# FFN up-projection in seven products of halves and four token blocks, in place of eight products and three blocks

## The chip, the cores and the metric

The kernel runs on one core of a Trainium2 chip. The metric is the device time of one execution in microseconds. Three runs of the kernel before took 3087.99, 3089.96 and 3090.21 us; the median, 3089.96 us, is the time before. The rows shown below come from one further execution under the profiler.

The engines by their names in the profile: PE is the matrix engine (PEld its weight loads), DVE the vector engine, ACT the scalar engine, POOL the GpSimd engine, SP the queue that issues most DMAs. Each engine works through its own instructions strictly in the order in which the kernel wrote them.

## The reference, cut to what matters

One decoder layer over 2048 prompt tokens and 8 sample tokens. The head part (a gated MLP over chunks, and an attention over a compressed cache) adds to `x`; then comes the part that is changed, a feed-forward net with a causal convolution of width 3:

```
def conv_ffn(x, conv_prev, g_ffn, w_up, w_conv, b_conv, w_down):
    h = rmsnorm(x, g_ffn)
    up = h @ w_up                                  # 1024 -> 2 x 2816 (gate and value)
    xp = jnp.concatenate([conv_prev, up], axis=1)
    c = b_conv
    for k in range(CONV_W):
        c = c + xp[:, k:k + T] * w_conv[k]
    gate, val = c[..., :D_FF], c[..., D_FF:]
    y = (jax.nn.silu(gate) * val) @ w_down         # 2816 -> 1024
    return y, xp[:, -(CONV_W - 1):]
```

The final result is `rmsnorm(x + y)`. All is float32.

## The kernel before, in words

Each float32 operand of a large product is split into a high and a low part in a shorter format, and a product is made of three matmuls: high by high, high by low, low by high (`mm3`, line 78). `split_to` (line 124) makes the two parts: ACT copies the high part out (line 86), and DVE or POOL subtracts it from the source (line 126).

The stages follow one another: latent projections (0 to 300 us), the gated MLP (300 to 560), the attention of the prompt (576 to 1106), the output projection (1106 to 1343), the feed-forward part (1343 to the end). In the gated MLP, `finish` writes its output to memory already split, a high and a low copy (`a_sp`, line 1021 on); the output projection reads both (`load_a`, line 1106).

The feed-forward part takes the tokens in three blocks (`BL`: 344 + 344, 344 + 344 and 424 + 256 tokens). For a block, `load_h2` brings the 1024 input rows in and splits them; each of 22 steps `fi` (in `up`, line 1769) then makes 128 gate and 128 value columns for both halves of the block. One half of one of these is 24 matmuls, 8 slices of the input by three, into one PSUM bank. `conv` (line 1567) takes the bank: DVE multiplies by the tokens' norm factor (line 1572), ACT writes two columns of the tokens before (line 1573), starts the convolution (line 1574) and saves the last two columns (line 1575), and DVE adds the other two taps (line 1577). `glu` applies the gate: silu on ACT, a product on DVE (line 1586), the high part on ACT, the low part on DVE. Three banks (`pu`) go round among the up-projections, three (`pd`) among the down-projections.

After two steps the down-projection of this pair is done, in eight pieces `m` for each half; a piece is six matmuls and a DVE addition to `y` (line 1597). `PIECES` says where among the next pair's up-projections a piece stands. The weights come in through POOL's DMA queue; ACT and POOL split them (1024 columns at a time, `split_w`, line 1366). At a block's end `ending` makes the last pair's down-projection, and the next block's input is prepared meanwhile.

Beside this runs the attention of the eight sample tokens over 16,384 cached positions: `fill` (line 869) counts the columns that were fed to PE and, when enough have passed, writes one more step of it between two matmuls. A step reads 4 pages for each of four samples; in the feed-forward part one stands after each 10.25 us of counted columns (at one column per 1/2.4 ns). It ends with the second block. In the third, `late` normalises the finished blocks' output. Nothing reorders what is written: the order in the code is the order on each engine.

## Time and profile before

| what | value |
| --- | --- |
| time, median of three runs | 3089.96 us |
| the profiled execution, its own time | 3097.86 us |
| its span, first to last instruction | 3096.1 us |
| PE busy, share of the span | 97% |
| DVE, ACT, POOL busy | 55%, 42%, 35% |
| feed-forward part | 1343 to 3096 us |
| PE's granted clock, mean | 0.987 |

"Busy" is the share of the span in which at least one instruction of the engine ran. PE's matmuls overlap one another, so what one matmul costs is read from the distance of starts in a row of them, not from the duration of one. In the groups of instructions a row gives busy time, mean duration of one, and the engine's idle time just ahead of them with the engine that ended it.

### The profile page before, as it was taken

Reading aid. Unit: us, or ns where it says so; the run is one execution under the profiler, and the core shown is the slowest. Engines: PE = TensorE matmul, PEld = TensorE weight load, DVE = VectorE, ACT = ScalarE, POOL = GpSimd, SP = SyncE. Lnnn points to the kernel's source line nnn. Section 1 sums busy time; section 2 is a strip of 40 time slices with the busy share of each in tenths; the row PEclk is TensorE's granted clock in tenths of the full one; section 3 lists DMA queues with packets and bytes.
Section 4 is the critical chain, followed back from the end, with each engine's and each line's share of the span. In section 5 each row is a group of like instructions: output and inputs, shape, how many; then the busy total and the mean of one; then the engine's idle time right before and its main releaser. Section 6 shows DMA issues by size and latency. Waiting matters only on the chain.

```text
span 3096.1 us, 66568 instructions
## 1 busy us (share of the span) xinstructions
PE 2992.7 (97%) x23814; PEld 2697.3 (87%) x23814; DVE 1716.6 (55%) x3595; ACT 1293.6 (42%) x2986; POOL 1088.1 (35%) x1097
## 2 busy tenths in 40 slices
PE   8999999999999989999999999999999999999997
PEld 7898788688887779879999999899898989999997
DVE  6466333577787754444444444554444456666666
ACT  5333333577778742233332322343332334444443
POOL 4342122422233234343333323333232334444442
PEclk9999999999999999999999999999999999999999
DMA  5446766788865789989777777949898845333333
GB/s 165 138 160 211 217 186 194 210 222 225 222 172 136 193 238 256 241 242 226 203 211 231 239 231 240 277 113 222 209 218 217 213 140 173 109 95 112 112 93 81
DMA packets 354070, 587.76 MB, mean 190 GB/s; under 512 B 60879, under 2 KB 261230, under 8 KB 353742
## 3 DMA queue, kind: packets, MB, share of 16 engines
q1 hardware_dynamic: 277520, 375.31, 43.6%
q0 software_dynamic: 56416, 197.65, 22.7%
q10 hardware_dynamic: 19806, 10.55, 1.1%
q8 instruction: 191, 3.13, 0.4%
q14 instruction: 137, 1.12, 0.1%
HBM read 515.50 MB, written 67.82 MB: 188 GB/s over the span
## 4 chain that ended last, share of the span: by engine, by line
PE 74%; DMA 8%; DVE 6%; issue 5%; ACT 4%; POOL 2%; SPq 1%; ACTq 0%; DVEq 0%; POOLq 0%
PE up L76 27%; PE dp L76 13%; PE s L76 5%; PE op L76 5%; PE sc L76 4%; PE po L76 4%; PE o L76 3%; PE t L1224 3%; PE pu L76 2%; PE pv L76 2%; DMA cn<-in_cN 2%; DMA ct<-in_cT 1%; SPq L66 1%; DVE c L1577 1%; PE pj L76 1%
## 5 line engine op out<-in xcount | busy, mean ns | idle before, releaser
L76 PE MATMUL up<-h,wu 128*128 128x344 f32 (+2 forms) x6336 | 1070.0, 321 | 6.1 <-DVE h L1550 2.1
L76 PEld LDWEIGHTS up<-h,wu 128*128 128x128 f32 x6336 | 1002.4, 189 | 22.0 <-issue 6.4
L126 POOL TENSOR_TENSOR wu<-wraw,wu 128x1024 fp32r<-128x1024 f32 x132 | 315.3, 2389 | 694.2 <-ACT wu L86 668.0
L1577 DVE SCALAR_TENSOR_TENSOR c<-up,gn,c 128x344 f32<-128x344 f32 (+2 forms) x528 | 302.6, 573 | 293.5 <-ACT halo L1575 284.2
L1573 ACT ACTIVATE up<-halo 128x2 f32<-128x2 f32 x264 | 46.1, 175 | 709.5 <-DVE up L1572 705.6
L76 PE MATMUL dp<-gh,wdh 128*128 128x344 f32 (+1 forms) x960 | 311.1, 324 | 12.3 <-ACT gh L86 6.4
L76 PE MATMUL dp<-gl,wdh 128*128 128x344 f32 (+1 forms) x960 | 306.9, 320 | 0.3
L76 PE MATMUL dp<-gh,wdl 128*128 128x344 f32 (+1 forms) x960 | 306.9, 320 | 0.0
L1597 DVE TENSOR_TENSOR y<-y,dp 128x344 f32<-128x344 f32 (+1 forms) x480 | 227.5, 505 | 118.5 <-PE dp L76 116.4
L1572 DVE TENSOR_TENSOR up<-up,R 128x344 f32<-128x344 f32 (+2 forms) x264 | 137.3, 520 | 232.6 <-PE up L76 232.4
L76 PE MATMUL s<-k,q 96*128 96x512 f32 (+2 forms) x960 | 254.0, 375 | 6.3 <-DMA k<-kr_sp 2.5
L126 POOL TENSOR_TENSOR wdl<-wraw,wdh 128x1024 fp32r<-128x1024 f32 x66 | 159.7, 2420 | 243.9 <-ACT wdh L86 237.7
L126 DVE TENSOR_TENSOR pl<-t,ph 128x512 fp32r<-128x512 f32 (+1 forms) x320 | 194.0, 606 | 50.7 <-ACT ph L86 47.1
L86 ACT ACTIVATE ph<-t 128x512 fp32r<-128x512 f32 (+1 forms) x320 | 170.2, 532 | 108.7 <-PE t L1224 104.2
L1212 ACT ACTIVATE S<-S,nm 128x512 f32<-128x512 f32 (+2 forms) x320 | 208.0, 650 | 7.1 <-POOL nm L1204 7.1
L76 PEld LDWEIGHTS s<-k,q 96*128 96x128 f32 x960 | 169.0, 191 | 45.4 <-DVE S L1200 6.6
L76 PEld LDWEIGHTS dp<-gh,wdh 128*128 128x128 f32 x960 | 181.3, 189 | 19.6 <-DVE y L1597 9.7
L76 PEld LDWEIGHTS dp<-gl,wdh 128*128 128x128 f32 x960 | 180.8, 188 | 2.3 <-DVE gl L126 1.4
L76 PEld LDWEIGHTS dp<-gh,wdl 128*128 128x128 f32 x960 | 180.9, 188 | 0.7
L1224 PE MATMUL t<-cst,S 128*128 128x128 f32 x1088 | 173.7, 274 | 2.3 <-DVE pl L126 2.2
L1574 ACT ACTIVATE c<-up,gn 128x344 f32<-128x344 f32 (+2 forms) x264 | 168.4, 638 | 8.9
L1224 PEld LDWEIGHTS t<-cst,S 128*128 128x128 f32 x1088 | 133.2, 140 | 35.0 <-DVE pl L126 7.1
(388 smaller groups left out, 5121.4 us busy)
## 6 DMA issues: line engine op xcount, KB each, us to landing
ct<-in_cT SPq DMA_DIRECT2D x1024, 144.0 KB
cn<-in_cN SPq DMA_DIRECT2D x1024, 128.0 KB
wraw<-in_w_up POOLq DMA_DIRECT2D x132, 512.0 KB, 4.8
wraw<-in_w_down POOLq DMA_DIRECT2D x66, 512.0 KB, 5.0
q_sp<-qs SPq DMA_DIRECT2D x48, 256.0 KB
ft<-x_sp SPq DMA_DIRECT2D x64, 172.0 KB
xt<-in_xT SPq DMA_DIRECT2D x16, 512.0 KB
kn_sp<-qs SPq DMA_DIRECT2D x32, 256.0 KB
```

What stands on the lines that cost most here:

```text
L66: return self.eng.dma_start(out=o, in_=i)
L76: pe.matmul(out, lhsT=w, rhs=x, start=start, stop=stop)
L86: act.activation(out, in_, AF.Copy)
L126: (lo_eng or dve).tensor_sub(lo, src, f(hi))
L1212: act.activation(s, s, AF.Exp, scale=SCALE, bias=d["nm"][:, qb:qb + 1], accum_out=d["ls"][:, qb, r:r + 1])
L1224: pe.transpose(p[:, (qb - q0) * 128:(qb - q0) * 128 + 128], d["S"][qb, kb // 4][:, ks], ident)
L1572: dve.tensor_mul(p[:, 2:2 + m], p[:, 2:2 + m], RT[b][:, o:o + m])
L1573: act.activation(p[:, 0:2], halo[:, ix, :], AF.Copy)
L1574: act.activation(c[:, 0:m], p[:, 2:2 + m], AF.Identity, scale=w[2], bias=g(B_CONV, ix))
L1577: dve.scalar_tensor_tensor(out=c[:, 0:npr], in0=p[:, j:j + npr], scalar=w[j], in1=c[:, 0:npr], op0=ALU.mult, op1=ALU.add)
L1597: dve.tensor_add(y, y, p[:, 0:nn])
```

## The change

The up-projection of a step `fi` is written as a product of two-by-two blocks: the weights' rows of blocks are gate and value, their columns the two halves of the input rows; the input's columns of blocks are the two token halves. Such a product of blocks needs eight products of halves; by Strassen's scheme (in Winograd's form) it is done with seven, of sums and differences of blocks. `split_w` makes the seven weight forms, of which four sums or differences are new work (two on DVE, two on POOL), and each form is split by ACT and POOL. `load_h2` makes the seven input forms once for a block, and multiplies the norm factor in there, so that `conv` no longer does. `up` adds the seven results together on DVE: `s1` (an ACT copy of the first result), `u2` and `u3` are kept in SBUF, the other sums are made in the PSUM banks.

A block has 512 tokens in halves of 256 (the last 520, halves of 260), and there are four blocks. A product of halves is 12 matmuls. The PSUM banks have fixed roles now: a, b, c and e for the seven products in the order a, b, a, b, c, b, e, one buffer each, and two for the down-projection, whose pieces are 512 tokens wide (in the last block two of 260). Weights come through SP's DMA queue, not POOL's. The gated MLP's output is stored once and split when it is read. The new query of the samples' second half is placed later in the sample stream, and `cnew` shares a buffer with the query.

```
-                split_to(a[:, 0], a[:, 1], p)
+                a = sb.tile([128, 4, 128], F32, tag="as" if c < 7 else ("hh", "hl")[tt], bufs=2, name="as")
+                copy(a, p)
...
                 if c < 7 or tt:
                     for a, t0 in todo:
-                        for i in range(2):
-                            aq.dma_start(out=a_sp[i, :, t0:t0 + 128].rearrange("(k p) t -> p k t", p=128), in_=a[:, i])
+                        aq.dma_start(out=a_sp[:, t0:t0 + 128].rearrange("(k p) t -> p k t", p=128), in_=a)
...
     def load_a(ci, tiles):
         MA[ci] = tiles
-        for i in range(2):
-            gq.dma_start(out=tiles[i], in_=a_sp[i, :, ci * CP:ci * CP + CP].rearrange("(k p) t -> p k t", p=128))
+        gq.dma_start(out=tiles[1], in_=a_sp[:, ci * CP:ci * CP + CP].rearrange("(k p) t -> p k t", p=128))
+
+    def split_a(ci, eng):
+        hi, lo = MA[ci]
+        copy(hi, f(lo))
+        eng.tensor_sub(lo, f(lo), f(hi))
 
...
+    FORMS = ("B11", "T2", "B21", "T3", "T1", "T4", "B22")
+    PIECES = ((0, 0, 1, 1, 1, 0, 0), (1, 1, 1, 1, 1, 0, 0))
+    BL = [(0, 256), (512, 256), (1024, 256), (1536, 260)]
+    NB, AHEAD = len(BL), 5
...
+    def form(src):
+        w = kslot([128, 2, 4, 128], "wu", F32R)
+        split_to(w[:, 0], w[:, 1], src, pool)
+        return w
...
+        A21, A22 = VAL[2 * q], VAL[2 * q + 1]
+        if j == 0:
+            src = A11
+        elif j == 1:
+            TMP[1] = sb.tile([128, 4, 128], F32, tag="t1", bufs=1, name="t1")
+            TMP[2] = sb.tile([128, 4, 128], F32, tag="t2", bufs=1, name="t2")
+            dve.tensor_add(TMP[1], A21, A22)
+            dve.tensor_sub(TMP[2], TMP[1], A11)
+            src = TMP[2]
+        elif j == 2:
+            src = A12
+        elif j == 3:
+            pool.tensor_sub(A21, A11, A21)
+            pool.tensor_sub(TMP[2], A12, TMP[2])
+            src = A21
         else:
-            gq.dma_start(out=t.rearrange("p j m n -> p j (m n)"),
-                         in_=A["w_down"][w[2] * 128:(w[2] + 2) * 128, w[3] * 512:w[3] * 512 + 512].rearrange("(j p) n -> p j n", p=128))
-        raw[w] = t
-
-    def split_w():
-        if at["split"] == len(order):
-            return
-        w = order[at["split"]]
-        at["split"] += 1
-        if w is None:
-            return
-        src = raw.pop(w)
-        if w[0] == "u":
-            hi, lo = (kslot([128, 8, 128], "wu", F32R) for _ in range(2))
...
+        wts[i] = form(src)
+        if j == 4:
+            later.append(load_g)
...
+            if i % (2 * NF) == 2 * NF - 2 or i == 4 * NU // 2 - 1:
+                w = kslot([128, 2, 2, 2, 128], "wd", F32R)
+                hi, lo = w[:, 0], w[:, 1]
+            else:
+                hi, lo = (sb.tile([128, 2, 2, 128], F32R, tag=t, name=t) for t in ("wdh", "wdl"))
+            split_to(hi, lo, DR.pop(i), pool)
+            wts["d", i] = hi, lo
+            dlater.append(load_d)
+
...
-        pd = mkpool(Fx, "f_pd", 3, PSUM)
+        pu = mkpool(Fx, "f_pu", 1, PSUM)
+        pd = mkpool(Fx, "f_pd", 2, PSUM)
         halo = one.tile([128, 2 * NF, 2], F32, name="halo")
...
+            hi("B21")
+            yield
+            lo("T2", dve)
+            hi("T3")
...
+            lo("T3", dve)
+            hi("T4")
+            yield
+            lo("T1", dve)
+            lo("T4", dve)
+            hi("B22")
+            yield
+            lo("B22", pool)
+            yield
 
         def load_y(b):
-            c0, n0, n1 = BL[b]
+            c0, hm = BL[b]
             for m in range(8):
...
-            c = sb.tile([128, 424], F32, tag=f"c{gv}", bufs=3 - gv, name=f"c{gv}")
-            dve.tensor_mul(p[:, 2:2 + m], p[:, 2:2 + m], RT[b][:, o:o + m])
+            c = sb.tile([128, 260], F32, tag=f"c{gv}", bufs=2, name=f"c{gv}")
             act.activation(p[:, 0:2], halo[:, ix, :], AF.Copy)
             act.activation(c[:, 0:m], p[:, 2:2 + m], AF.Identity, scale=w[2], bias=g(B_CONV, ix))
             act.activation(halo[:, ix, :], p[:, npr:npr + 2], AF.Copy)
...
                     dve.tensor_add(y, y, p[:, 0:nn])
                     fill(6 * nn / 2.4)
-                    yield
+                if m % 2:
+                    dlater.append(split_d)
+                yield
 
         def wide(name):
...
         def up(b, fi, it, side, slow, hs):
-            halves = ends(b)
-            cg = []
-            for gv in range(2):
-                wh, wl = wts.pop(("u", b, fi, gv))
-                both = fi == gv == 0
-                for h, (o, m) in enumerate(halves):
-                    at_k, at_end = (ENDING if fi == NF - 1 and b == 2 else PIECES)[4 * (fi % 2) + 2 * gv + h]
-                    if not (both and o):
-                        ps = [pu.tile([128, 512], F32, tag="u", name="up") for _ in range(1 + both)]
-                        for k in range(8):
-                            for p, (o_, m_) in zip(ps, halves if both else ((o, m),)):
-                                mm3(p[:, 2:2 + m_], [(wh[:, k, :], wl[:, k, :], h2[b][0][k][:, o_:o_ + m_], h2[b][1][k][:, o_:o_ + m_])], k == 0, k == 7)
...
-                                take(side, 1 + both)
-                            if k == 3 and not both:
...
+
+            def prod(j, name):
+                w, (xh, xl) = wts.pop(7 * q + j), H[FORMS[j]]
+                ps[name] = p = pu.tile([128, 512], F32, tag="u" + name, name="up")
+                for k in range(4):
+                    mm3(p[:, 2:2 + hm], [(w[:, 0, k, :], w[:, 1, k, :], xh[:, k, 0:hm], xl[:, k, 0:hm])], k == 0, k == 3)
+                    fill(3 * hm / 2.4)
+                return p[:, 2:2 + hm]
+
+            def rest(j):
+                todo, later[:] = later[:], []
+                dtodo, dlater[:] = dlater[:], []
+                for fn in todo + dtodo:
+                    fn()
+                while at["w"] <= 7 * q + j + AHEAD and at["w"] < 7 * NU:
+                    split_w()
+                take(it, PIECES[odd][j])
+                take(side, 1)
+                take(slow, 1)
+                take(hs, 1)
+
+            s1, u2, u3 = (sb.tile([128, 260], F32, tag=t, bufs=1, name=t)[:, 0:hm] for t in ("s1", "u2", "u3"))
+            copy(s1, prod(0, "a"))
+            rest(0)
+            dve.tensor_add(u2, s1, prod(1, "b"))
+            rest(1)
+            p = prod(2, "a")
+            dve.tensor_add(p, s1, p)
+            cg = conv(b, fi, 0, ps["a"], 0, hm)
+            rest(2)
+            dve.tensor_add(u3, u2, prod(3, "b"))
+            rest(3)
+            p = prod(4, "c")
+            dve.tensor_add(u2, u2, p)
+            dve.tensor_add(p, u3, p)
+            rest(4)
+            p = prod(5, "b")
+            dve.tensor_add(p, u3, p)
+            cv = conv(b, fi, 1, ps["b"], 0, hm)
+            if odd:
+                take(it, 99)
+            gt = [sb.tile([128, 520], F32R, tag=t, bufs=3, name=t) for t in ("gh", "gl")]
+            run(glu(cg, cv, gt, 0, hm))
+            cv = conv(b, fi, 1, ps["c"], hm, hm)
+            rest(5)
+            p = prod(6, "e")
+            dve.tensor_add(p, u2, p)
+            cg = conv(b, fi, 0, ps["e"], hm, hm)
+            last = glu(cg, cv, gt, hm, hm)
+            next(last)
+            if not (b == NB - 1 and fi == NF - 1):
+                run(last)
+            rest(6)
             return gt, last
 
...
+        for b in range(NB):
...
+                if fi == NF - 1 and b < NB - 1:
+                    if b == NB - 2:
+                        drain()
+                    hs = load_h2(b + 1)
+                gt, last = up(b, fi, it, side, slow if fi else none, hs)
...
-                act.activation(sb.tile([128, 1], F32, tag="t1", bufs=1, name="t1"), epst, AF.Sqrt)
+            split_d()
+            if b < NB - 1:
+                it = ending(b, (before, gt))
+                for _ in range(8):
+                    take(it, 1)
+                    take(hs, 1)
```

ACT's order, at the end of a step and the start of the next. In the kernel before, a stretch of a step's two value halves (`wu` is a weight's high part, `up<-halo` starts a conv, `c` its first tap or, `c<-c`, the silu, `gh` the gated result's high part):

```order
L86 ACTIVATE wu<-wraw 128x1024
L1573 ACTIVATE up<-halo 128x2
L1574 ACTIVATE c_26294<-up,gn 128x344
L1575 ACTIVATE halo<-up 128x2
L1585 ACTIVATE c_26098<-c_26098 128x344
L86 ACTIVATE gh<-c_26294 128x344
L1573 ACTIVATE up<-halo 128x2
L1574 ACTIVATE c_26450<-up,gn 128x344
L1575 ACTIVATE halo<-up 128x2
L1585 ACTIVATE c_26138<-c_26138 128x344
L86 ACTIVATE gh<-c_26450 128x344
L86 ACTIVATE wu<-wraw 128x1024
```

And in the changed kernel, the end of a step with odd `fi` (the convolutions of banks c and e, `wdh` a down weight's high part, `s` the next step's `s1`):

```order
L1741 ACTIVATE up<-halo 128x2
L1742 ACTIVATE c_24734<-up,gn 128x256
L1743 ACTIVATE halo<-up 128x2
L86 ACTIVATE wdh<-draw 128x512
L86 ACTIVATE wu<-vraw 128x512
L1741 ACTIVATE up<-halo 128x2
L1742 ACTIVATE c_24763<-up,gn 128x256
L1743 ACTIVATE halo<-up 128x2
L1753 ACTIVATE c_24763<-c_24763 128x256
L86 ACTIVATE gh<-c_24734 128x256
L86 ACTIVATE wu<-t_24665 128x512
L86 ACTIVATE s_24778<-up 128x256
```

Two weight copies stand between the two convolutions now, and the copy of the next step's first product, which gives bank a free for its third, stands behind the whole of the gate.

POOL's order. In the kernel before, among the up-projections (`wu` and `wdl` are low parts):

```order
L126 TENSOR_TENSOR wu<-wraw,wu 128x1024
L66 DMA wraw<-in_w_up 128x1024
L126 TENSOR_TENSOR wu<-wraw,wu 128x1024
L66 DMA wraw<-in_w_down 128x2x512
L126 TENSOR_TENSOR wu<-wraw,wu 128x1024
```

In the changed kernel, at the end of a step with odd `fi` (lines 1397 and 1398 are the two differences of the next weight forms):

```order
L126 TENSOR_TENSOR wu<-graw,wu 128x512
L126 TENSOR_TENSOR wdl<-draw,wdh 128x512
L1397 TENSOR_TENSOR vraw<-graw,vraw 128x512
L1398 TENSOR_TENSOR t_26786<-graw,t_26786 128x512
L126 TENSOR_TENSOR wu<-vraw,wu 128x512
L126 TENSOR_TENSOR wu<-t_26785,wu 128x512
```

The DMA issues are gone from POOL, its subtractions are half as wide and more than twice as many, and the difference `vraw`, which ACT's copy `wu<-vraw` reads, stands behind the low part of a down weight.

## Rows read from the trace of the kernel before

**Rows 1.** The page, its first two lines (span; busy us, share, instructions).

```profile
span 3096.1 us, 66568 instructions
...
PE 2992.7 (97%) x23814; PEld 2697.3 (87%) x23814; DVE 1716.6 (55%) x3595; ACT 1293.6 (42%) x2986; POOL 1088.1 (35%) x1097
```

**Rows 2.** Busy by stage: length; PE, PEld, DVE, ACT, POOL; PE clock, DMA share, GB/s.

```profile
300.00:560.00 260.00, 251.01 (x1918) 202.79 (x1917) 90.95 (x207) 90.36 (x162) 62.53 (x85) 0.97 0.71 206
1140.00:1342.00 202.00, 195.68 (x1698) 179.36 (x1691) 79.44 (x117) 43.96 (x92) 83.05 (x106) 0.97 0.92 245
1400.00:1900.00 500.00, 500.00 (x4857) 477.63 (x4856) 237.24 (x498) 150.91 (x359) 169.58 (x113) 1.00 0.78 224
2690.00:3050.00 360.00, 354.09 (x2251) 344.92 (x2250) 227.69 (x471) 149.38 (x359) 157.95 (x112) 1.00 0.35 103
```

**Rows 3.** The chain of waits, whole run; columns: start, us, what.

```profile
363.44 5.58 PE pv L76 x24
...
1328.35 14.40 PE op L76 x120
...
1440.67 11.33 PE up L76 x72
...
2684.32 11.22 PE up L76 x72
```

**Rows 4.** Timeline of PE around 1702 us; columns: start, us, engine, what.

```profile
1702.19 1.95 PE L76 MATMUL sc<-ct,qz 128*32 128x128 f32 x64
...
1704.30 2.15 PE L76 MATMUL up<-h,wu 128*128 128x344 f32 x12
```

**Rows 5.** Timeline of DVE and ACT, one half of 256, third block.

```profile
2923.46 0.43 DVE L1572 TENSOR_TENSOR up<-up,R 128x256 f32<-128x256 f32 x1
...
2923.98 0.17 ACT L1573 ACTIVATE up<-halo 128x2 f32<-128x2 f32 x1
2924.19 0.56 ACT L1574 ACTIVATE c<-up,gn 128x256 f32<-128x256 f32 x1
2924.65 0.16 ACT L1575 ACTIVATE halo<-up 128x2 f32<-128x2 f32 x1
2924.85 0.99 DVE L1577 SCALAR_TENSOR_TENSOR c<-up,gn,c 128x248 f32<-128x248 f32 x2 [0.96 <-ACT halo L1575]
...
2925.94 0.41 ACT L1585 ACTIVATE c<-c 128x256 f32<-128x256 f32 x1
...
2927.06 0.42 DVE L1586 TENSOR_TENSOR c<-c,c 128x256 f32<-128x256 f32 x1
...
2927.51 0.42 ACT L86 ACTIVATE gh<-c 128x256 fp32r<-128x256 f32 x1 [1.16 <-DVE c L1586]
...
2927.96 0.42 DVE L126 TENSOR_TENSOR gl<-c,gh 128x256 fp32r<-128x256 f32 x1 [0.48 <-ACT gh L86]
```

**Rows 6.** Groups by form, 0 to 1345 us, POOL, ACT and DVE.

```profile
L126 POOL TENSOR_TENSOR vl<-gv,vh 128x512 fp32r<-128x512 f32 x16 | 20.7, 1291 | 24.5 <-ACT vh L86 24.5
...
L86 ACT ACTIVATE ph<-t 128x256 fp32r<-128x256 f32 x32 | 12.3, 384 | 10.9 <-PE t L1224 10.4
...
L86 ACT ACTIVATE vh<-gv 128x512 fp32r<-128x512 f32 x16 | 10.1, 631 | 27.6 <-DVE gv L1058 27.6
...
L1115 DVE TENSOR_TENSOR rd<-rd 128x512 f32<-128x512 f32 x7 | 4.9, 700 | 10.4 <-ACT rd L1114 10.4
```

**Rows 7.** Timeline of POOL and DVE around 1370 us.

```profile
1369.58 2.38 POOL L126 TENSOR_TENSOR wu<-wraw,wu 128x1024 fp32r<-128x1024 f32 x1
1369.84 2.50 DVE L1586 TENSOR_TENSOR c<-c,c 128x344 f32<-128x344 f32 x1 [0.61 <-ACT c L1585]
```

**Rows 8.** Timeline of PE around a gap at 1107 us.

```profile
1106.23 0.92 PE L76 MATMUL op<-ma,wo 128*128 128x256 f32 x6
1111.24 6.79 PE L76 MATMUL op<-ma,wo 128*128 128x256 f32 x42 [4.09 <-DVE rdT L1256]
```

**Rows 9.** Busy time and clock behind this gap; columns as in rows 2.

```profile
1110.00:1114.00 4.00, 2.76 (x13) 2.76 (x14) 3.76 (x6) 0.00 (x0) 1.97 (x4) 0.67 0.19 41
```

More of the change, by code (lines that the diff above doesn't have):

```diff
@@ L765, in sample_stream @@
             yield 1500
+            if s == 0:
+                qz = yield from place_q(1)
             def turned(p0):
@@ new lines, in build, with load_g, load_v @@
+    PIECES = ((0, 0, 1, 1, 1, 0, 0), (1, 1, 1, 1, 1, 0, 0))
+    BL = [(0, 256), (512, 256), (1024, 256), (1536, 260)]
+    NB, AHEAD = len(BL), 5
+    NU = NB * NF
+    GATE, VAL, TMP, wts, later, dlater = {}, {}, {}, {}, [], []
+    at = {"g": 0, "v": 0, "w": 0, "dl": 0, "ds": 0}
+    def load_g():
+        q = at["g"]
+        at["g"] += 1
+        if q < NU:
+            GATE[q] = qslot([128, 8, 128], "graw")
+            (sp if q else gq).dma_start(out=GATE[q], in_=A["w_up"][q % NF, 0])
+    def load_v():
+        if not at["v"]:
+            at["v"] = 2
+            t = qslot([128, 8, 128], "vraw")
+            gq.dma_start(out=t, in_=A["w_up"][0, 1])
+            VAL[0], VAL[1] = t[:, 0:4], t[:, 4:8]
+            return
+        q, a = divmod(at["v"], 2)
+        at["v"] += 1
+        if q < NU:
+            VAL[2 * q + a] = t = sb.tile([128, 4, 128], F32, tag="vr", bufs=3, name="vraw")
+            sp.dma_start(out=t, in_=A["w_up"][q % NF, 1, :, 4 * a:4 * a + 4, :])
@@ new lines, in load_h2 @@
+                lo("T2", dve)
+                for n, eng in (("B21", dve), ("T3", pool), ("T1", dve), ("T4", pool), ("B22", dve)):
+                    hi(n)
+                    lo(n, eng)
+                return
+            free("B11")
+            sp.dma_start(out=raw("B11"), in_=src(0, 4, 0))
+            R = load_r()
+            yield
+            free("T2")
+            yield
+            free("B21")
+            sp.dma_start(out=raw("B21"), in_=src(4, 4, 0))
+            yield
+            free("T3")
@@ new lines, in load_h2 @@
+            sp.dma_start(out=raw("T3"), in_=src(0, 4, 1))
+            yield
+            free("T1")
+            for k in range(4):
+                scale(raw("B11", k), raw("B11", k), k, 0)
+            yield
+            free("T4")
+            xs = temps()
+            for i in range(2):
+                sp.dma_start(out=xs[i], in_=src(4 + 2 * i, 2, 1))
+            for k in range(4):
+                scale(raw("B21", k), raw("B21", k), 4 + k, 0)
+            yield
+            free("B22")
@@ new lines, in load_h2 @@
+            for k in range(4):
+                scale(raw("T3", k), raw("T3", k), k, 1)
+            hi("B11")
+            yield
+            sub("T1", "T3", "B11", dve)
+            yield
+            for k in range(4):
+                scale(b22(k), b22(k), 4 + k, 1)
+            lo("B11", pool)
+            yield
+            sub("T2", "B22", "T1", dve)
+            hi("T2")
+            yield
+            sub("T4", "B21", "T2", pool)
+            sub("T3", "B22", "T3", dve)
+            hi("B21")
@@ new lines, in ending @@
+            for i in (0, 1, 2, 3, 4, 8, 9, 5, 10, 11, 12, 13, 6, 14, 7, 15):
+                m = i % 8
+                if i < 8:
+                    ps[m] = bank(m)
+                    part(m, 0)
+                    continue
+                part(m, 1)
+                y = Y[b][m][:, 0:512]
+                dve.tensor_add(y, y, ps.pop(m))
+                sp.dma_start(out=x3_sp[m * 128:(m + 1) * 128, BL[b][0]:BL[b][0] + 512], in_=y)
+                if m % 2 and m != 5:
+                    split_d()
+                    while dlater:
+                        dlater.pop(0)()
@@ L1637, in late @@
+            for o in range(0, 1536, 512):
+                cols = slice(o, o + 512)
                 t = load(0)
@@ L1894, in build @@
-            assert next(slow, 0) == 0
-            it, slow = none, late() if b == 1 else none
+            take(it, int(TA))
+            r0 = root(0)
+            for _ in range(4):
+                take(r0, 1)
+                take(it, 1)
+            take(r0, 9)
+            take(it, 99)
+            for m in DA0:
+                scale(0, m, dve, sp)
+            half = [scale_pool(0, m, sp) for m in range(8) if m not in DA0 + DA1]
+            for t in half:
+                next(t)
+            r1 = root(1)
@@ L1896, in build @@
+            take(r1, 1)
+            for t in half:
+                next(t, 0)
+            take(r1, 99)
+            for m in DA1:
+                scale(0, m, dve, sp)
+            for m in range(8):
+                scale(1, m, pool if m in DA2 else dve, aq if m % 2 else sp)
     smp.close()
```

413 lines of the change are left out of this document (204 added, 209 removed).

## Prediction

> **What bounds the kernel now.** I read the page's busy shares first: PE works for 97% of the span [rows 1], so PE's stream is the time. The table by stage says where that holds: in the first block of the feed-forward part PE is busy for all 500 of 500 us, in the third for 354 of 360, with DVE at 47% and 63%, POOL at 34% and 44% [rows 2]. The other engines are servants with slack: what they do ends in time, and only columns fed to PE count. The change takes PE work away and gives DVE, ACT and POOL more, so the question is whether they still end in time. For that I read the chain of waits for the price of a matmul [rows 3] and the timeline of one convolution for the delay from a full bank to the finished gate [rows 5].
>
> **PE work removed.** Cost of a matmul by its width, from runs in the chain of waits [rows 3]: 256 columns 14.40/120 = 0.120 us; 344 columns 11.33/72 = 0.157; 424 and 256 in equal number 11.22/72 = 0.156 on average; 512 columns 5.58/24 = 0.2325. Before, up: 4224 x 0.157 + 2112 x 0.156 = 994 us. Now each of 88 steps has 7 products of 12 matmuls: 7392 x 0.120 = 887 (a quarter of them have 260 columns: +3). Down: 3168 matmuls at 0.157 and 0.156 = 497 before; now 1584 of 512 columns and 1056 of 260: 368 + 128 = 496. The sum is -105 us; of the nominal 1/8 of the columns a part goes into 1056 more matmuls. Were this all, the time would be 3098 - 105 = 2993. The sample stream's steps, 2.11 us each on PE [rows 4], stay as many; in a pair of steps 28.16 us of columns are counted now, so 28.16/10.25 = 2.75 sample steps stand in a pair, 5.8 us.
>
> **The new wait.** Call the end of a step's sixth product (bank b) zero. Bank a takes the step's first and third product, so the next step's third waits for the ACT copy `s1`. PE has only the seventh product and the next step's first and second before it: 3 x 12 x 0.120 = 4.3 us; after an even step two down pieces of 6 x 0.2325 = 1.4 us more, 7.1 us. But ACT and DVE have three convolutions and two gates to do first, in a fixed order, each waiting for the other. From one half of 256 tokens [rows 5]: a DVE operation on a bank 0.42; ACT's three operations until DVE starts 0.87; the two taps 0.99; silu 0.41, product 0.42, high part 0.42. Walk: sum for bank b done at 0.5; its taps from 1.5 to 2.5; product 2.9; high part 3.35; ACT then takes bank c, its taps run from 4.1 to 5.1, and only behind them comes DVE's sum for bank e, 5.5; taps from 6.45 to 7.45; silu 7.9; product 8.3; high part 8.75; a weight copy, 0.63 [rows 6]; `s1`, 0.38 [rows 6]: 9.6 us. PE has 4.3 or 7.1 us of work for it, and on average one sample step per pair.
>
> After an odd step POOL enters the chain. Between c and e ACT copies a down weight (to 4.6); POOL's low part of it and then the difference `vraw` are 1.29 us each [rows 6], to 7.2; ACT's copy `wu<-vraw` waits for that and ends at 7.85, and e's convolution, due at 5.6, starts there: `s1` at 11.9. After an even step the first gate's product meets POOL at the same two differences. Rows show what that costs: a product of 344 that started 0.26 us behind a POOL subtraction took 2.50 us, and ended 0.38 us after it [rows 7], against 0.42 for 256 alone [rows 5]. For a POOL operation of 1.29 I take half of it: 10.2.
>
> From `s1` on, the third to sixth product and three pieces take 4 x 1.44 + 3 x 1.4 = 10 us on PE, so that a step is about 20 to 22 us and sample steps, where PE alone would need 16.
>
> Per pair in blocks one to three PE stands still for (11.9 - 4.3) + (10.2 - 7.1) - 2.1 = 8.6 us.
>
> The clock adds to this. Behind a gap of 4.09 us at 1107 us [rows 8] the granted clock of the next stretch is 0.67 [rows 9], and 42 matmuls took 6.79 us, where 42 x 0.120 = 5.04: 1.75 us lost, 1.2 in place of 2.4 GHz for a part of them. The gap after an odd step (7.6) is longer than that one, the other (3.1) shorter; I take 1.75 once and half of it once, 2.6 per pair.
>
> 33 pairs x 11.2 = 370; the first pair of each of these blocks has no pieces and costs 3.3 more: 380. Block four has no sample steps, pieces of 12 x 0.120 = 1.45 us, and two short DVE operations for the sample columns in banks c and e (1 us a step; unmeasured at this place, 0.5 to 1.5): per pair 7.5 + 2.9 + 2 + 3.5 (both gaps are long there) = 15.9, times 11 = 175. Sum 555.
>
> **The rest.** At a block's end the last gate of the odd step is late by some 10 us and DVE has seven subtractions of 1024 columns for the next block's input, while PE has only the down-projection of the last pair. I put 10 us for each of three block ends and 10 for the start, where the norm factor is now on the way to the first matmul: 40, within 0 (all of it in PE's shadow) and 80. Weights by SP's queue, which has pages to issue: the weights are asked for about a step ahead, and PE needs 512 tokens' worth of them more slowly than before; nothing, 0 to 20. The gMLP output stored once: PE idles for 9.0 us in that stage and 6.3 in the output projection [rows 2], so nothing above 15 can come back; split when read, it puts an ACT copy and a POOL subtraction of 1024 columns before each chunk's norm, beside eight pieces of 2.9 us of PE work; between -15 and +10, I take 0. The sample's query and `cnew` moved: nothing.
>
> **Sum.** 3098 - 105 + 555 + 40 = 3588 for a profiled execution; the profiled one before was 8 us above the median of the runs, so 3580.
>
> **Rivals.**
>
> A lighter chain: the same wait, but POOL does not come into it and the gaps leave the clock alone. Then both tails are 9.6: (19.2 - 11.4 - 2.1) x 33 + 10 + 7.5 x 11 = 281, no cost at block ends, 3098 - 105 + 281 - 8 = 3266. For it: POOL is busy for only 22 x 1.29 = 28.4 us of a pair of 40 or more. Against it: the order puts POOL's two operations into the odd tail whatever its share, and the clock did fall behind a gap. This floor needs no unmeasured number.
>
> A heavier one: DVE falls behind too. In the middle of a step it has two sums of weights, 0.70 each alone [rows 6]; if each meets a POOL operation by half, 1.3 us a step reaches the sixth sum, 114 in all; the other half of the clock's price (30) and the normalisation of finished blocks in block four (33) come on top: 3757. Against it: that stretch is PE's, and after a gap PE is slower itself, so much of the 1.3 is covered.
>
> Not slower: PE never waits, since the tails are covered; 2985. The place is bank a, and it decides at a tail of 4.3 to 7.1 us plus a sample step; the walk would have to be too long by half. For it: before, the same convolutions are wholly hidden, with PE at 500 of 500 us [rows 2]. Against: there the four halves of a step come 3.8 us or more apart, as PE makes them (24 x 0.157), now three come within 1.44 us and ACT may not pass one by. In this case block four has a bound of its own, DVE and POOL together: if their operations on two SBUF tensors can't overlap [rows 7], a pair has 28.4 of POOL and 8 x 0.42 + 4 x 0.70 = 6.2 of such DVE work, 34.6 us, against 264 x 0.1217 = 32.1 on PE; 11 x 2.5 = 28 us, and the time is 3013. The Trainium skill, "SBUF — State Buffer", section "SBUF: two separate sides", states it as a rule: a VectorE operation with two SBUF inputs and a GpSimd operation that reads SBUF share one pair of ports, and the later one is blocked for the whole of the earlier. The 2.50 us row agrees with it.
>
> That the change does not do what it says is no case: the order shows 12 matmuls a product, seven products a step.
>
> **Chances.** The forecast's chain (3400 to 3700) 0.6; the lighter 0.18; the heavier 0.13; not slower 0.09. The range from 3290 to 3750 leaves out the last, the lowest part of the lighter and the top of the heavier. This kernel's runs agree within 0.1%, so 0.2% or 6 us can be told from no change: faster 0.08, the same 0.01, slower 0.91.
>
> **What would show it.** Right: PE's share falls to about 80%, its idle time stands ahead of the third product of each step (waiting for ACT's `s1`), longer after odd steps; ACT waits for POOL at `wu<-vraw` in odd steps for some 2.5 us, for DVE at `gh` and `up`; the clock's mean falls to about 0.93; steps in the middle of blocks one to three last about 24 us on average, up matmuls start 0.120 us apart within a product. Wrong: PE stays above 95%, or its idle time stands elsewhere (behind DMA, at block ends, at pieces). Were ACT's copy `s1` to end less than 7 us after the sixth product, the whole sum falls.

## The result and the profile after

The changed kernel takes 3665.23 us (median of 4 runs, 3660.63 to 3672.88), the kernel before 3090.09 (4 runs, 3087.99 to 3092.2): 1.186 times as long, 95% interval 1.184 to 1.189. Forecast were 3580 us, range 3290 to 3750. Each time of an experiment below is that of one run where no number of runs stands with it.

The head of the page after (span, then busy us, share and instructions), to be read against [rows 1]:

```profile
span 3662.3 us, 71440 instructions
...
PE 3040.3 (83%) x24340; PEld 2651.6 (72%) x24340; DVE 2120.6 (58%) x4367; ACT 1627.3 (44%) x4025; POOL 1770.5 (48%) x1665
```

PE now stands still for 3662.3 - 3040.3 = 622 us; before it was 103 [rows 1]. It is also busy for 48 us more, although the counted work fell by 105: some 153 us went into slower matmuls, most of it to the lower clock, as shown further down. These two, 518 and 48, are the whole change of the span.

The table by stage (length; PE, PEld, DVE, ACT, POOL; PE clock, DMA share, GB/s) says where. The first window is the gated MLP, where only the store of its output is changed, and has its like in the first line of [rows 2]; the others lie in the first block and in block four:

```profile
300.00:560.00 260.00, 252.66 (x1938) 203.30 (x1937) 83.69 (x198) 92.81 (x166) 65.30 (x87) 0.97 0.67 196
1400.00:1900.00 500.00, 406.78 (x3624) 355.52 (x3624) 266.30 (x541) 196.23 (x530) 280.10 (x222) 0.89 0.63 187
3100.00:3550.00 450.00, 311.69 (x2224) 303.90 (x2225) 277.85 (x603) 191.77 (x502) 254.12 (x195) 0.83 0.30 99
```

PE was busy for 500 of 500 us in the first block [rows 2], now for 407, and DVE, ACT and POOL are at 62% or less in each of the windows: no engine is busy all the time. The view of waits names who waits for whom (engine, its instruction's line, releaser: us in total, times, longest):

```profile
PE up L76 <- ACT s L86: 366.5, 73, 11.7
...
ACT wu L86 <- POOL vraw L1397: 106.3, 40, 4.2
...
PE dp L76 <- DVE y L1769: 69.9, 20, 7.6
...
DVE t L1391 <- DMA vraw<-in_w_up: 32.5, 11, 5.6
```

The first line is the forecast's wait: 366.5 us ahead of `up` for ACT's copy `s1`. All of it stands ahead of a step's third product (input form `B21h`), as the group of these matmuls shows (busy us, mean ns, idle time ahead and its releaser):

```profile
L76 PE MATMUL up<-B21h,wu 128*128 128x256 f32 (+1 forms) x704 | 211.0, 376 | 366.5 <-ACT s L86 366.5
```

The second line is ACT's wait for POOL's difference, 2.66 us each; all 40 stand between the sixth product of an odd step and the next `s1`. The third, down pieces that wait for DVE, was not in the forecast; all but 0.3 us of it is in block four.

Here is one odd tail of the third block, from the timeline (start us, us, engine, what), first PE, then ACT, POOL and DVE:

```profile
2716.00 0.28 PE L76 MATMUL up<-T4h,wu 128*128 128x256 f32 x1
2716.12 0.29 PE L76 MATMUL up<-B22h,wu 128*128 128x256 f32 x1
...
2728.14 0.58 PE L76 MATMUL up<-B21h,wu 128*128 128x256 f32 x1 [5.52 <-ACT s L86]
2728.52 0.42 PE L76 MATMUL up<-B21l,wu 128*128 128x256 f32 x1
2728.74 0.63 PE L76 MATMUL up<-B21h,wu 128*128 128x256 f32 x2
```

```profile
2719.28 0.42 ACT L86 ACTIVATE gh<-c 128x256 fp32r<-128x256 f32 x1 [1.36 <-DVE c L1754]
...
2720.31 0.63 ACT L86 ACTIVATE wdh<-draw 128x512 fp32r<-128x512 f32 x1
2723.55 0.63 ACT L86 ACTIVATE wu<-vraw 128x512 fp32r<-128x512 f32 x1 [2.61 <-POOL vraw L1397]
2724.09 0.16 ACT L1741 ACTIVATE up<-halo 128x2 f32<-128x2 f32 x1
...
2726.88 0.42 ACT L86 ACTIVATE gh<-c 128x256 fp32r<-128x256 f32 x1 [0.49 <-DVE c L1754]
...
2727.72 0.36 ACT L86 ACTIVATE s<-up 128x256 f32<-128x256 f32 x1
```

```profile
2721.02 1.28 POOL L126 TENSOR_TENSOR wdl<-draw,wdh 128x512 fp32r<-128x512 f32 x1 [4.93 <-ACT wdh L86]
2722.25 1.27 POOL L1397 TENSOR_TENSOR vraw<-graw,vraw 128x512 f32<-128x512 f32 x1
...
2724.70 1.26 POOL L126 TENSOR_TENSOR wu<-vraw,wu 128x512 fp32r<-128x512 f32 x1
```

```profile
2716.32 0.43 DVE L1987 TENSOR_TENSOR up<-u,up 128x256 f32<-128x256 f32 x1 [0.73 <-PE up L76]
...
2724.93 1.00 DVE L1745 SCALAR_TENSOR_TENSOR c<-up,gn,c 128x256 f32<-128x256 f32 x2 [3.14 <-ACT halo L1743]
```

The sixth product's last matmul (form `T4h`) starts at 2716.00 and ends at 2716.28. Counted from there, the first high part is done at 3.4 us, ACT's copy of the down weight at 4.7, POOL's difference at 7.2, ACT's copy that waited for it at 7.9, the second high part at 11.0, `s1` at 11.8. The prediction's walk had 3.35, 4.6, 7.2 and 7.85 for the first four and 11.9 for the last. PE had a sample step beside its 4.3 us of work here and still stood still for 5.52 us.

Behind that gap the granted clock is at its lower level: 0.50, 1.2 GHz in place of 2.4, in the 4 us after it (the column ahead of the last two). The price: matmuls of 256 columns start 0.22 us apart there (2728.52 to 2728.74) in place of 0.12. It is the case of [rows 8, 9] again.

```profile
2728.00:2732.00 4.00, 3.86 (x15) 3.67 (x16) 0.85 (x2) 1.63 (x6) 3.66 (x3) 0.50 1.01 224
```

### The profile page after: what moved, and what is told of

It reads as the page before. It is cut to its first block, busy times and chain, and to the rows that moved or that the text cites. A ratio compares the mean times of both kernels' runs of the same rounds, so it can differ in the third digit from the quotient of the medians.

```text
span 3662.3 us, 71440 instructions
## 1 busy us (share of the span) xinstructions
PE 3040.3 (83%) x24340; PEld 2651.6 (72%) x24340; DVE 2120.6 (58%) x4367; ACT 1627.3 (44%) x4025; POOL 1770.5 (48%) x1665
## 5 line engine op out<-in xcount | busy, mean ns | idle before, releaser
L126 POOL TENSOR_TENSOR wu<-t,wu 128x512 fp32r<-128x512 f32 x264 | 345.4, 1308 | 510.5 <-ACT wu L86 486.2
L1745 DVE SCALAR_TENSOR_TENSOR c<-up,gn,c 128x256 f32<-128x256 f32 (+2 forms) x704 | 340.7, 484 | 372.5 <-ACT halo L1743 359.9
L76 PE MATMUL up<-B21h,wu 128*128 128x256 f32 (+1 forms) x704 | 211.0, 376 | 366.5 <-ACT s L86 366.5
L76 PE MATMUL dp<-gh,wdh 128*128 128x512 f32 (+1 forms) x800 | 305.4, 382 | 70.4 <-DVE y L1769 69.9
L126 POOL TENSOR_TENSOR wdl<-draw,wdh 128x512 fp32r<-128x512 f32 x171 | 228.6, 1337 | 254.9 <-ACT wdh L86 249.3
L76 PE MATMUL dp<-gl,wdh 128*128 128x512 f32 (+1 forms) x800 | 299.4, 374 | 0.0
L76 PE MATMUL dp<-gh,wdl 128*128 128x512 f32 (+1 forms) x800 | 297.2, 371 | 0.0
L126 POOL TENSOR_TENSOR wu<-vraw,wu 128x512 fp32r<-128x512 f32 x176 | 229.8, 1306 | 116.5 <-ACT wu L86 116.5
L126 POOL TENSOR_TENSOR wu<-graw,wu 128x512 fp32r<-128x512 f32 x176 | 228.2, 1297 | 103.6 <-ACT wu L86 103.6
L1741 ACT ACTIVATE up<-halo 128x2 f32<-128x2 f32 x352 | 59.3, 169 | 477.2 <-DVE up L1987 217.1
L1769 DVE TENSOR_TENSOR y<-y,dp 128x512 f32<-128x512 f32 (+1 forms) x400 | 226.6, 577 | 59.4 <-PE dp L76 58.5
```

What stands on the lines that cost most here:

```text
L76: pe.matmul(out, lhsT=w, rhs=x, start=start, stop=stop)
L126: (lo_eng or dve).tensor_sub(lo, src, f(hi))
L1741: act.activation(p[:, 0:2], halo[:, ix, :], AF.Copy)
L1745: dve.scalar_tensor_tensor(out=c[:, 0:npr], in0=p[:, j:j + npr], scalar=w[j], in1=c[:, 0:npr], op0=ALU.mult, op1=ALU.add)
L1769: dve.tensor_add(y, y, p[:, 0:nn])
```

## The experiments

The theory is the prediction's: bank a waits for `s1`, and `s1` stands behind a serial chain of ACT and DVE into which POOL comes in odd steps; the clock falls behind the gaps. Its rivals: the mere amount of ACT's and DVE's work, or a clock that falls for another reason. "Tail" is the time from the end of the sixth product to the end of the next `s1`, a mean over the fifth to twentieth step of a block; in the changed kernel it is 9.8 to 10.4 us after even and 12.1 to 12.6 after odd steps of blocks one to three, 12.2 and 13.8 in block four.

**The second gate behind `s1`.** Only the place of the work changes, not its amount.

```diff
 copy(s1, prod(0, "a"))
+take(gate2[0], 1)      # of the step before: conv of c, sum for e
 ...
 dve.tensor_add(u2, s1, prod(1, "b"))
+take(gate2[0], 99)     # of the step before: conv of e, gate
 ...
-cv = conv(b, fi, 1, ps["c"], hm, hm)
 rest(5)
 p = prod(6, "e")
-dve.tensor_add(p, u2, p) ... run(last)
+gate2[0] = second(b, fi, ps, u2, gt)
```

(shortened; a block's last step keeps the old order)

> Changed kernel with the second value convolution (bank c), the last sum (bank e), its convolution and the second gate of a step emitted behind the next step's copy s1 (not in the last step of a block). Theory (ACT's and DVE's serial tail in front of s1 is what PE waits for): after an even step s1 comes within 5 us of the sixth product, PE has 7.1 us of work, no wait; after an odd step POOL's difference still holds ACT up to about 7, s1 at 8.2 in place of 11.8, and the first down piece of the pair now waits some 3 us for the late gate. So the waits behind even steps go (2 us a pair with their clock in blocks one to three, about 7 in block four) and those behind odd steps are mostly moved: about 3510, between 3430 and 3560. Rival (PE waits for ACT's and DVE's mere amount of work, not for its place): no change, 3640 to 3690.

Measured: 3515.38 us, inside what was expected. The tails are 5.0 to 5.8 us after even steps and 9.0 to 9.2 after odd ones in blocks one to three. The wait for `s1` shrank, and there is a new one of the down pieces for the late gate's high part:

```profile
PE dp L76 <- ACT gh L86: 78.2, 37, 4.4
...
PE up L76 <- ACT s L86: 70.8, 22, 4.3
...
PE up L76 <- ACT up L1741: 68.0, 20, 6.7
```

The third line stands ahead of the third product too (`up` of L1741 is what ACT writes right behind `s1` here): with the second it makes 139 us in place of 366.5, nearly all of it behind odd steps. The amount of ACT's and DVE's work is nearly the same (DVE 2099.8 us busy, ACT 1630.6; 2120.6 and 1627.3 in the changed kernel), so the rival on amounts is out.

**POOL out of the tail.** The two differences are issued one product earlier.

```diff
 elif j == 2:
+    pool.tensor_sub(A21, A11, A21)
+    pool.tensor_sub(TMP[2], A12, TMP[2])
     src = A12
 elif j == 3:
-    pool.tensor_sub(A21, A11, A21)
-    pool.tensor_sub(TMP[2], A12, TMP[2])
     src = A21
```

> Changed kernel with POOL's two differences (vraw and t2) emitted one product earlier, out of the tail. Theory: ACT's wait for POOL in odd steps (2.66 us, 40 times) goes, the tail behind an odd step shrinks from 11.8 to about 9.6, s1 comes 2.2 us earlier in 44 steps, and the gate's product in even steps no longer meets POOL (0.6): -100 to -125, about 3550. Rival (POOL's difference is only moved in front of another copy that waits for it, or the clock decides): less than 20 us either way, 3645 to 3680.

Measured: 3603.03 us, 62 less. ACT's wait for POOL is gone from the list of waits, and the odd tail is 9.95 to 10.94 us in blocks one to three: about 2 us shorter, as expected. The even tail is not (9.9 to 11.0). So POOL's part in the odd tail is shown, but little more than half of the expected gain came, less than the range. In even steps the gate's product still meets POOL: the low part `wu` now stands where the two differences stood, and the first gate product of an even step takes 0.90 us in the mean of the fifth to twentieth steps (0.92 in the changed kernel), where one that meets no POOL operation takes 0.43.

```profile
PE up L76 <- ACT s L86: 288.0, 74, 9.7
```

**Both.**

> Both edits together: second half's convolutions and gate behind the next step's s1, and POOL's differences a product earlier. Theory: s1 about 5.6 us behind the sixth product after an odd step (PE has 4.3), within PE's work after an even one; of the old stand the wait of the first down piece of a pair for the late gate is left, about 4 us in every even step: about 3420, between 3340 and 3500. The gain is more than the sum of the two apart. Rival (amount of DVE and ACT work): 3550 or more.

Measured: 3441.43 us, inside the range: 224 less, against 150 and 62 apart. They add; the 12 us on top, which the expectation had wanted, are no more than the spread of the changed kernel's runs. The tails are 5.0 to 6.7 us. The largest part of what is left stands ahead of the first down piece of a pair:

```profile
L76 PE MATMUL dp<-gh,wdh 128*128 128x512 f32 x480 | 201.4, 420 | 77.5 <-ACT gh L86 73.3 <-DVE y L1769 4.2
...
L76 PE MATMUL up<-B21h,wu 128*128 128x256 f32 x528 | 114.1, 296 | 38.1 <-ACT s L86 18.4 <-ACT up L1741 18.3 <-DMA draw<-in_w_down 1.0
...
L76 PE MATMUL dp<-gh,wdh 128*128 128x260 f32 x320 | 102.1, 319 | 95.8 <-ACT gh L86 53.7 <-DVE y L1769 41.9
```

(Groups by form: count, busy us, mean ns, idle time ahead and its releasers.) In the changed kernel the third product's group, 256 wide, has 270.8 us of idle time from 1345 us on, where it has 38.1 here.

**The gMLP output stored once, alone,** put into the kernel before.

```diff
-a_sp = dram.tile([2, 512, SEQ], F32, name="a_sp")
+a_sp = dram.tile([512, SEQ], F32, name="a_sp")
 ...
-split_to(a[:, 0], a[:, 1], p)
+copy(a, p)
```

(shortened; with `load_a` and `split_a` as in the change)

> Kernel before, with the gMLP output alone stored once in place of twice (split when it is read). Forecast of the prediction's step: no change, between -15 and +10 us against the kernel before. Rival: the halved store and load speeds up the output projection and shows as over 6 us.

Measured: 3075.36 us (6 runs) against 3090.73 (11 runs), ratio 0.9944, 95% interval 0.9922 to 0.9966: faster by 11 to 24 us, as the rival had it; the prediction's step had put it at nothing. In the output projection, PE's largest wait before, and the same wait with this edit:

```profile
PE po L76 <- DMA cn<-in_cN: 8.4, 4, 3.9
```

```profile
PE po L76 <- DMA cn<-in_cN: 1.0, 1, 1.0
```

The whole stage, from the first product to the first matmul of the feed-forward part:

```profile
1106.20:1344.70 238.50, 224.01 (x1930) 203.98 (x1929) 96.98 (x143) 56.15 (x112) 98.45 (x126) 0.96 0.91 244
```

```profile
1102.20:1325.00 222.80, 217.54 (x1928) 201.65 (x1928) 97.54 (x143) 61.89 (x119) 112.35 (x126) 0.99 0.91 243
```

The stage is 15.7 us shorter: PE stands still for 9.2 us less in it and is busy for 6.5 us less, at a clock of 0.99 for 0.96. The DMA engines are at 0.91 in both and move 244 and 243 GB/s, with 4 MB less to read in the stage (the 4 MB less to write belong to the gated MLP's). At 243 GB/s these 4 MB are 17 us, an estimate that comes near the 15.7. My reading is that the sample stream's `cn` now comes in time and that the clock no longer falls behind its gaps; no run parts the fewer bytes from the moved instructions. This version beats both kernels.

**The wait filled.** PE gets 52 matmuls of no use ahead of the third product of an even step.

```diff
 rest(1)
+if not odd and fi:
+    p = pd.tile([128, 512], F32, tag="d", name="fill")
+    w, xh = last_w[0], H["B11"][0]
+    for _ in range(52):
+        mm(p[:, 0:hm], w[:, 0, 0, :], xh[:, 0, 0:hm], True, True)
 p = prod(2, "a")
```

> Changed kernel with 52 matmuls of no use (256 or 260 columns, result read by nobody) ahead of the third product of each even step but a block's first, 6.2 us where PE stands still for 7 to 9. Theory: the lower clock behind the gap comes of the standing still; with PE at work the 1.85 us lost behind each of 40 such gaps come back: -60 to -85, about 3590. Rival (the clock has another cause, or its loss is covered by ACT's and DVE's chain): -20 to +40.

Measured: 3617.98 us, 47 less; expected were 60 to 85. The granted clock of 1400 to 1900 us, 0.89 in the changed kernel, is now 0.97:

```profile
1400.00:1900.00 500.00, 452.20 (x4199) 399.43 (x4197) 280.87 (x563) 201.88 (x537) 289.03 (x228) 0.97 0.64 191
```

2080 more matmuls at 0.120 are 250 us, but PE is busy for 179 more (3219.6): some 71 us of slow work came back, and the end comes 47 us earlier. A kernel that does more work is faster because of it, and the clock stays up where PE no longer stands still: so the rival of another cause for the clock is out.

**Block four.** The final normalisation of the first three blocks is left out (`slow = none` for `slow = late()`).

> Changed kernel without the final normalisation of the first three blocks that runs beside block four (it leaves out these columns of the output). Theory: block four's excess over the forecast (tails 12.2 and 13.8 us in place of 10.2 and 11.9) comes half from the two short operations for the sample columns and half from this work on ACT and DVE: -20 to -60, about 3625. Rival (the excess is the wait of the second piece's bank for DVE, and has nothing to do with it): 0 to -10.

Measured: 3647.47 us, 18 less, just short of what was expected: a part of block four's excess, and little. Block four's tail after even steps falls from 12.2 to 10.9 us, the one after odd steps from 13.8 to 13.5. Then the second down piece of odd steps, moved there from behind the second product to behind the fifth.

```diff
-take(it, PIECES[odd][j])
+take(it, (1, 0, 1, 1, 2, 0, 0)[j] if odd and b == NB - 1 else PIECES[odd][j])
```

> Changed kernel with the second down piece of odd steps in block four moved from behind the second product to behind the fifth. Theory: this piece covers nothing in block four, since its halves take the two banks whose additions to y wait on DVE behind the tail (64 us of waits, 18 times), and is worked off behind s1 instead; elsewhere it costs nothing: -10 to -18, and the waits for y are gone. Rival (it does cover): +10 to +20.

Measured: 3655.68 us (4 runs, 3653.44 to 3658.81), 10 less; the ratio to before, 1.1829 with 1.1806 to 1.1853, overlaps the changed kernel's interval, so that a gain is not clear of the noise. What the wait was, from the changed kernel's PE:

```profile
3293.41 0.59 PE L76 MATMUL dp<-gh,wdh 128*128 128x260 f32 x1 [7.64 <-DVE y L1769]
```

and where it stands here, the down piece first:

```profile
L76 PE MATMUL dp<-gh,wdh 128*128 128x260 f32 x320 | 98.5, 308 | 1.8 <-DVE y L1769 1.5
...
L76 PE MATMUL up<-B21h,wu 128*128 128x260 f32 x176 | 62.8, 433 | 159.9 <-ACT s L86 159.9
```

The wait for `y` is gone, but nearly all of it stands ahead of the third product now (159.9 us, 95.7 in the changed kernel): the same tail under another name.

**Towards a faster version: five that went wrong or halfway.** All build on the two edits together. First, other places for sums, weight copies and pieces (cut to the main lines):

```diff
-PIECES = ((0, 0, 1, 1, 1, 0, 0), (1, 1, 1, 1, 1, 0, 0))
+PIECES = ((0, 0, 0, 0, 1, 1, 1), (1, 1, 1, 1, 1, 0, 0))
 ...
+first = glu(cg, cv, gt, 0, hm)
+next(first)    # silu, product
+splits(5)      # weight copies here
+run(first)     # high and low part
```

> Like e3_both, and: the sum for bank e stays in its own step; two weight copies of ACT stand between a gate's silu and its high part (where ACT waits for DVE's product), the third behind the next step's s1; both late convolutions follow s1 back to back; the third sum u3 stands ahead of the first gate convolution; the down pieces of even steps stand two products later (after products 5, 6 and 7). Theory: s1 about 4.3 us behind the sixth product, the late gate's high part at about 9, first piece of a pair at 9 or later: PE stands still for 1 to 2 us a pair in place of 5, the clock stays up; blocks one to three 39 to 40 us a pair (e3_both: 43.5), block four 40 (47.7): about 3205, between 3150 and 3290. Rival (DVE's amount of work binds, 30 us a pair with waits between): above 3350.

Measured: 3486.76 us, 45 more than with the two edits and no others: some 200 us above the range. `s1` does come 5 to 6 us behind the sixth product after odd steps, but the even tail is 9.8 to 10.8 again and the waits stand elsewhere:

```profile
DVE t L1391 <- DMA vraw<-in_w_up: 180.1, 40, 9.7
...
PE dp L76 <- DVE y L1769: 130.3, 64, 8.8
```

Then the pieces alone moved, to ((0, 0, 0, 0, 3, 0, 0), (0, 0, 1, 2, 2, 0, 0)), and, in a second kernel, the weight loads asked for at once as well (`while later: later.pop(0)()` behind each split):

> Like e5_reorder, with the down pieces placed elsewhere: in even steps all three behind the fifth product, in odd steps none behind the first two, then 1, 2, 2. In e5_reorder s1 came 5 us behind the sixth product after an odd step as meant, but four pieces in a row stood in the tail of the even step, where their two banks wait for additions to y queued on DVE behind the gate (dp for y: 130 us). Theory: these waits go, a pair in blocks one to three takes 39 to 40 us (e5_reorder 43.7) and one in block four 43 (50.7): 3487 - 135 - 85, about 3270, between 3200 and 3340. Rival (late loads of the weights hold DVE, 180 us at t from vraw, and with it everything else): 3400 or more.

> Like e8_pieces, with weight loads asked for right behind the split that frees their buffer (not one product later) and the split of the fifth product's weight two products earlier. If DVE's wait for vraw matters: 60 to 120 below e8_pieces; if it is only idle time of DVE off the path: within 20 of it.

Measured: 3658.48 and 3534.87 us. All tails are short now (4.7 to 7.9 us), and the first is as slow as the changed kernel, some 320 us above its range: the pieces' wait for `y` grew to 228.5 us, and DVE's wait for `vraw` stayed at 185.6. My reading of the run before, that four pieces in a row were the trouble, fell. The loads at once, together with one weight split two products earlier, are worth 124 us: DVE's wait for `vraw` falls to 20.6 us and the pieces' for `y` to 156.8. The rows agree with this account: DVE takes its work in order, and the sums `t` that need `vraw` stand ahead of the additions to `y` that free the pieces' two banks.

Last, both edits with the even steps' pieces one product later, ((0, 0, 0, 1, 2, 0, 0), ...), and the same with loads at once:

> Like e3_both, with the down pieces of even steps one product later (0, 1, 2 behind the third, fourth and fifth product become 0, 1, 2 behind the fourth and fifth: none, one, two). In e3_both PE stands still ahead of the first piece of a pair for the late gate's high part (127 us in 39 waits). Theory: PE now has one product more to do, that wait shrinks by up to 2.9 us in 44 steps, the later products still find their sums in time: -90 to -150, about 3320. Rival (as in e5_reorder and e8_pieces the pieces then wait for additions to y, which DVE does late): 3400 to 3500.

> Like e11_later, with each weight load asked for right behind the split that frees its buffer. DVE waits for vraw 63 us in e3_both, 19 times. Theory: a late vraw holds DVE's sums and with them the additions to y, so that part of it comes back: -10 to -60 against e11_later. Rival (idle time of DVE off the path, and SP now waits for POOL): within 15 of it, or slower.

Measured: 3484.84 and 3432.75 us. The first is 43 us slower than the two edits with no others, as its rival had it: the pieces' wait for the high part went as meant (127 us to under 8, in the two forms together), and a wait for `y` took its place:

```profile
L76 PE MATMUL dp<-gh,wdh 128*128 128x512 f32 x480 | 198.7, 414 | 65.3 <-DVE y L1769 59.4 <-ACT gh L86 5.8
...
L76 PE MATMUL dp<-gh,wdh 128*128 128x260 f32 x320 | 110.3, 345 | 81.4 <-DVE y L1769 79.6 <-ACT gh L86 1.4
```

Loads at once gave 52 us, inside what was expected. 3432.75 us is the lowest time with seven products, 11% above the kernel before and not clearly below the 3441.43 of the two edits. What its pieces still wait for is DVE (125 us for `y`); whether for the amount of DVE's work or for its order isn't shown.

## Why the prediction was right, and by how much it was low

**Bounds and PE's work: right.** With PE at 97% the other engines had time to spare; what decided was the order of their work, where the forecast looked for it. A product takes 12 x 0.120 us where the clock is up, as costed. The 105 us stand by count and spacing alone: PE's busy time can't show them, since the clock took more back.

**The new wait: right, to 0.1 us in the odd tail shown.** In the means of blocks one to three the even tail is within 0.4 us of the walk (9.8 to 10.4 for 10.2) and the odd one 0.2 to 0.7 longer (12.1 to 12.6 for 11.9). Place (third product), cause (`s1`), and the difference between odd and even steps are all in the rows above, and moving the tail's work moved the wait with it. PE stands still for 8.1 to 10.0 us a pair in blocks one to three; the term was 8.6.

**POOL in the chain: right.** In the odd tail shown ACT waits 2.61 us for POOL, 2.66 in the mean (some 2.5 forecast), and the run that took POOL out of the tail shows it. For even steps the forecast charged half of a POOL operation to the first gate's product, some 0.6 us. The changed kernel's own trace gives the measure: a first gate product of an even step takes 0.92 us in the mean of the fifth to twentieth steps, 0.5 more than one that meets no POOL operation. One of them, on POOL and DVE:

```profile
1558.52 1.28 POOL L1398 TENSOR_TENSOR t<-graw,t 128x512 f32<-128x512 f32 x1
```

```profile
1559.01 1.07 DVE L1754 TENSOR_TENSOR c<-c,c 128x256 f32<-128x256 f32 x1
```

A product of 0.42 [rows 5] took 1.07 and ended 0.28 us behind POOL's operation, much as in [rows 7]. The Trainium skill, "SBUF — State Buffer", section "SBUF: two separate sides", has it that a VectorE operation with two SBUF inputs and a GpSimd operation that reads SBUF exclude each other for a whole instruction; the trace agrees. The taps, which read a bank and SBUF, took their usual 1.00 us at 2724.93 although POOL was at work (from 2724.70 on).

**The clock: right.** The spacing of matmuls behind the gaps gives about 2.5 to 2.9 us lost a pair in blocks one to three (term: 2.6) and 3.9 in block four (term: 3.5). PE's mean granted clock is 0.907; some 0.93 was forecast.

**Low by 77 us in the sum.** Measured against the sum for a profiled execution, 3588: PE stands still for 518 us more than before, 470 were summed (284 + 10 in blocks one to three, 136 in block four, 40 for the start and the block ends); slower matmuls took some 153, 124 were summed. The term of block four, "7.5 + 2.9 + 2 + 3.5", was mis-sized most: 16.2 us of standing a pair and 3.9 of clock make 20.1 in place of 15.9, 46 us over 11 pairs. Two things were not in that term: a piece there has two halves that take both banks `d`, so a second piece covers little while DVE is in the tail (some 10 us, not clear of the noise), and the normalisation of finished blocks (18 us), which only the heavier rival had, at 33. The rest, some 18 us, stays open. The 1 us a step for the sample columns' two operations, called unmeasured there, holds: with the normalisation left out, block four's tails are 0.8 and 1.1 us longer than the means of the other blocks. Block ends and start cost more than 40, though less than the 80 that were their bound: PE stands still for 21.0, 18.5 and 22.2 us in the last steps of blocks one to three and 17.0 in the very first step. A little luck helped the number: the feed-forward part starts at 1334.4 us in place of 1344.7, a gain ahead of it that the sum had put at nothing; without it the measured time would have been some 10 us further above the sum.

**The gMLP store: the choice of 0 was wrong.** 15.4 us came back (11 to 24), at the far end of the -15 to +10 that were given. The bound of 15 counted PE's idle time alone; in the output projection 9.2 us of idle time came back and 6.5 us of busy time, at a higher clock.

**SP's queue: little cost here, as said,** by the rows (32.5 us of DVE's waits); no run tested it on the changed kernel itself. In two of the later versions late loads were worth 52 and 124 us.

**The rivals.** The lighter chain failed on POOL and the clock, both in the rows. The heavier one's mechanism did not come: DVE's sum starts 0.04 us behind the end of the sixth product in all but four of the 48 steps looked at (the fifth to twentieth of blocks one to three), and at most 0.24 behind it in block four. Of its prices the normalisation came, at 18 us for 33. Not slower, the third, failed on bank a: PE is busy for 83% of the span.

## What to carry to other kernels

When a change removes PE work, walk the chain from each full bank to the instruction that frees it, in the order that each engine takes its work, and compare it with the PE work issued in between; busy shares of 40 to 60% did not show it here. Here a chain of cheap instructions cost more than the saved columns gave, and moving a part of it brought back 224 us without taking any work away. Four of the versions above mended one wait and met another in its place, so ask for each moved instruction what stands behind it on its in-order engine.

## What the runs showed of the hardware that I had not expected

A kernel with 250 us of useless matmuls was 47 us faster than the one without: behind the wait of 5.52 us TensorE was granted 1.2 GHz in place of 2.4 for its next work (0.50 in the 4 us shown), and the losses by spacing from a step's third to its sixth product were 0.6 to 2.9 us behind waits of 5 to 8 us (fifth to twentieth steps of blocks one to three), and only 0.1 to 0.3 behind waits of about 1 us.

Less traffic of one stream went with shorter waits for another: with the gMLP output stored once, PE's wait for the sample stream's loads `cn` fell from 8.4 to 1.0 us at a nearly unchanged rate (244 and 243 GB/s), and that stage, in which no wait of PE before names the gMLP's loads, became 15.7 us shorter.

A VectorE product of two SBUF tensors that met a running GpSimd subtraction ended 0.28 us behind it, while the taps, with one input in PSUM, were not slowed: the 341 that met a GpSimd operation for over 0.1 us and the 356 that met none took 0.48 us in the mean alike.
